# Attention products in halves of the TensorE array, and outputs that come out transposed

## The chip, the cores and the metric

The kernel runs on one core of one Trainium2 chip. The metric is the device time of one launch in microseconds: the median of the runs. Inside the core, TensorE multiplies, VectorE, ScalarE and GpSimd (POOL) work on elements, and DMA queues move data between device memory and the on-chip buffer SBUF. TensorE writes to PSUM, which has eight banks of 512 float32 columns on 128 partitions. The profile's PE is TensorE, PEld its loading of weights (the operand that stays in the array), DVE is VectorE and ACT ScalarE.

## The reference

A trunk of two residual layers for 256 tokens of 2048 features, all in float32. What matters here is the attention:

```python
# even layer, mixer A: 16 latent heads; an indexer of 16 heads of 64 features picks 64 keys per query
dots = relu(einsum('bqhd,bsd->bqhs', qi_b, k_idx))
score = einsum('bqh,bqhs->bqs', wi_b, dots) * idx_scale      # causal, then top-k
logits = einsum('bqhc,bqkc->bhqk', q_b, kv_sel) * att_scale + bias
o = softmax(logits) @ kv_sel, then @ w_uv                     # 64 features per head
# even layer, mixer B: 16 heads of 64 features, a window of 128 keys, two key/value heads, a sink logit
logits = q @ k / 8 + bias;  probs = softmax([logits, sink])[..., :-1];  o = probs @ v
# odd layer, mixer C: 32 heads of 64 features, causal, with a decay from forget gates
logits = q @ k / 8 + decay;  o = softmax(logits) @ v
# each layer:  x += concat(o) @ w_out;  x += conv_ffn(norm(x));  x += sigmoid(norm(x) @ w_gate) * (p @ w_proj)
```

## The kernel before

Tokens are handled in two blocks of 128 (`b` = 0, 1); in block `b` a query sees `n` = 128 or 256 keys. Weights come from device memory in pieces (`load`, L102), and `granule` splits each into two parts, `whi` on ScalarE (L114) and `wlo` on VectorE (L115). A large product is then three products in the parts, which `Acc.add` (L142) and the feed-forward part (L808, L810) issue. Products between activations in the attention stay in plain float32, and each of them appears in the trace as two instructions with a weight load each.

`attention` (L231) handles some heads of one token block. `head_groups` (L219) divides the heads into groups that fill one PSUM bank: four heads of 128 keys or two of 256. Where a head has 64 features, two heads share a tile of 128 partitions, and a group holds either the even heads (partitions 0 to 63) or the odd ones (64 to 127); the groups follow one another. For each group `front` makes the scores (L246) in the one bank of the ring `qk`, adds the bias or decay on VectorE, takes the maximum (L252), and exponentiates on ScalarE (L254) with the sums on the side. `back` transposes the probabilities (L263) into a bank of the ring `ax`, copies them out (L266), and multiplies them with the values (L269): the probabilities are the weights, the 64 columns of a value head stream, and the outputs [tokens, heads x 64] gather in the one bank `o`. The front of the next group is issued ahead of the back of the last. At the end VectorE takes the reciprocals of the sums (L282) and multiplies the outputs by them while it copies them out (L283). `transpose_split` (L165 to L171) transposes the outputs again, four 128x128 tiles per 512 columns (L169), and splits them for the output projection. The index scores (L462 to L473) have the same order of groups, with a relu in place of the softmax.

The eight banks are four rings: `mm` 3, `o` 1, `qk` 1, `ax` 3. The up-projections of the feed-forward part take banks from `mm` and `qk` in turn. `ple_project` (L752) multiplies the per-layer embedding before the feed-forward part, from two buffers of its own.

The program doesn't fix the order on each engine by its text alone: a planner orders the instructions by a simulated time and by priority. Attention is issued at a raised priority, so TensorE's order puts its pieces between the products of the projections, which fill the time in which other engines work on a score. Each engine then runs its list in order.

Of the kernel before, what the change touches and what calls it, by code (L numbers as in the profile page):

```python
# [16 lines left out]
P = 128  # L17
# [25 lines left out]
BANKS = dict(mm=3, o=1, qk=1, ax=3)  # L43
# [3 lines left out]
def trunk(ctx, tc, t, onehot, out):  # L47
# [20 lines left out]
    def rsqrt(dst, src, n, scale, post=1.0):  # L68
        """dst = post / sqrt(src * scale + EPS), by Newton from an exponent guess; [P, NT, n] or [P, NT]"""
# [54 lines left out]
    class Acc:  # L124
        """PSUM accumulators [tokens, ncols] of both token blocks for one column chunk."""
# [52 lines left out]
    def norm(gain, name, loaded=()):  # L178
        """Transposes of x * gain; 1 / rms is left to the caller (h.rstd), on the products."""
# [17 lines left out]
    def bcast_cols(dst, cols):  # L197
        """dst[:, token] = cols[block][token in block], on every partition of dst"""
# [6 lines left out]
    def transpose_to(dst, src, n, parts=P, scale=None, eng="v"):  # L205
        """dst [128, n*parts-token] <- n transposed [parts, 128] column tiles of src."""
# [12 lines left out]
    def head_groups(nh, n, halves):  # L219
        """Local head indices, as many as a PSUM bank holds; where two heads share a column tile  # L220
        (halves), the heads of the lower and the upper partitions go to different banks."""
        per = 512 // n
        if not halves:
            return [list(range(g, min(g + per, nh))) for g in range(0, nh, per)]
        gs = []
        for g in range(0, nh, 2 * per):
            m = min(g + 2 * per, nh)
            gs += [list(range(g, m, 2)), list(range(g + 1, m, 2))]
        return gs

    def attention(pool, heads, b, qk, logits, vv, y_out, halves, extra=0, mask=None):  # L231
        """Writes y_out [tokens, heads * 64] for token block b."""
# [4 lines left out]
        nl = sm.tile([P, 8], F32, tag="att_l", name="att_l", bufs=2)[:, :nh]  # L237

        def front(grp):
            per = len(grp)  # L240
            ps = psum("qk")
            s = pool.tile([P, 516], F32, tag="att_s", name="att_s", bufs=3)[:, :per * (n + extra)].rearrange("p (h c) -> p h c", h=per)
            for i, m in enumerate(grp):
# [3 lines left out]
            for i, m in enumerate(grp):  # L247
                logits(s[:, i, :], ps[:, i * n:(i + 1) * n], heads[m], b, n)
            if mask is not None:
                nc.vector.tensor_tensor(s[:, :, :n], s[:, :, :n], mask[:, None, :n].to_broadcast([P, per, n]), op=ALU.add)  # L250
            nm = sm.tile([P, 4], F32, tag="att_m", name="att_m", bufs=3)[:, :per]
            nc.vector.tensor_reduce(nm, s, axis=AX.X, op=ALU.max, negate=True)  # L252
            for i, m in enumerate(grp):
                nc.scalar.activation(s[:, i, :], s[:, i, :], AF.Exp, bias=nm[:, i:i + 1],  # L254
                                     accum_out=nl[:, m:m + 1])
            return s

        def back(grp, s):
            per = len(grp)
            pt = psum()  # L260
            for i in range(per):
                for kb in range(nk):
                    nc.tensor.transpose(pt[:, (i * nk + kb) * P:(i * nk + kb + 1) * P],  # L263
                                        s[:, i, kb * P:(kb + 1) * P], ident)
            pT = pool.tile([P, 512], F32, tag="att_p", name="att_p", bufs=2)
            nc.scalar.copy(pT[:, :per * n], pt[:, :per * n])  # L266
            for i, m in enumerate(grp):
                for kb in range(nk):
# [4 lines left out]
        grps = head_groups(nh, n, halves)  # L273
        prev = None
        for grp in grps:
            s = front(grp)
            if prev is not None:
                back(*prev)
            prev = grp, s
        back(*prev)  # L280
        rl = sm.tile([P, 8], F32, tag="att_r", name="att_r", bufs=2)[:, :nh]
# [8 lines left out]
    def ssq_heads(pool, ps, nh, dst):  # L290
        """dst [P, nh] = per-head sums of squares of ps [P, nh*64]."""
# [16 lines left out]
    # ======================= even layer: DSA + sliding window ====================  # L308
    def even_mixer(i, e):
        W = t["w_in_even"][e]  # L310
        with ExitStack() as es:
            ev = es.enter_context(tc.tile_pool(name="ev", bufs=1))
            def bias_tile(h0, nh):
                """[P, nh, 256]: column m of a row i is the bias of distance i + m - 127."""
# [5 lines left out]
            def key_bias(toe, m, n):  # L320
                """bias of the last n of 256 keys for head m of a bias tile, in the order of the keys"""
# [3 lines left out]
            # the first loads, in the order of their use  # L325
# [10 lines left out]
            # --- c_q  # L336
# [27 lines left out]
            # relative-position bias vectors: rv[h, m] = bias of distance m - 127  # L364
# [7 lines left out]
            for m in range(2):  # L372
                pr = psum()
                nc.tensor.matmul(pr[:16, :RV], tab[:, m * 16:(m + 1) * 16], oh[:, m, :], start=True, stop=True)
                rv = ev.tile([P, 516], F32, tag="att_s", name="rv", bufs=3)[:16, :RV]
# [3 lines left out]
            # --- c_kv, k_idx, w_idx  # L379
# [18 lines left out]
            for b in range(NT):  # L398
# [3 lines left out]
                # the index keys twice, so that both halves of the partitions hold them  # L402
# [14 lines left out]
            # --- index queries (features on partitions), scores, top-k masks  # L417
# [36 lines left out]
            with tc.high_priority(offset=PR):  # L454
                for b in range(NT):
                    n = P * (b + 1)
                    acc = ev.tile([P, S], F32, name=f"score{b}")
                    # causal mask first: keys after the query rank behind all others
# [3 lines left out]
                    for grp in head_groups(IDX_H, n, True):  # L462
                        pd = psum("qk")
                        for m, hh in enumerate(grp):
                            q0 = (hh % 2) * HD
                            nc.tensor.matmul(pd[:, m * n:(m + 1) * n], qiT[hh // 8][q0:q0 + HD, (hh % 8) // 2, b * P:(b + 1) * P],  # L466
                                             kiT[q0:q0 + HD, :n], start=True, stop=True)
                        rl = ev.tile([P, 516], F32, tag="att_s", name="relu", bufs=3)[:, :512]
                        nc.scalar.activation(rl, pd, AF.Relu)
                        for m, hh in enumerate(grp):  # L470
                            nc.vector.scalar_tensor_tensor(acc[:, :n], rl[:, m * n:(m + 1) * n],
                                                           wix[b][:, hh:hh + 1], acc[:, :n],
                                                           op0=ALU.mult, op1=ALU.add)  # L473
# [8 lines left out]
            # --- keys and values of the sliding window heads  # L482
# [27 lines left out]
            # --- values of the latent heads: kv @ w_uv  # L510
# [13 lines left out]
            # --- latent heads  # L524
            ya = {}

            def att_a(c):
# [10 lines left out]
                for b in range(NT):  # L538
# [5 lines left out]
                    if c % 2:  # L544
                        transpose_split(yT, c // 2, b, ya[b])

            # --- sliding window heads
# [15 lines left out]
            def att_b(c, qbT, rqs):  # L563
# [11 lines left out]
                for b in range(NT):  # L575
# [3 lines left out]
                    transpose_split(yT, 2 + c, b, y)  # L579
# [27 lines left out]
    # ============================ odd layer: forgetting attention ==================  # L607
    def odd_mixer(i, o):
        W = t["w_in_odd"][o]
        HDC = H_C * HD  # L610
        with ExitStack() as es:
# [44 lines left out]
            def att(g, qT, rqs, kT, v):  # L656
# [34 lines left out]
            # forget gates, heads on partitions  # L691
# [8 lines left out]
            # scratch for the gates, in the buffers of the first heads  # L700
# [11 lines left out]
            # log1p(e) = ln(u) + (e - (u - 1)) / u with u = fl(1 + e)  # L712
# [207 lines left out]
```

## Time and profile before

| | |
|---|---|
| median of 3 runs | 2465.46 us (2464.89 to 2466.26) |
| profiled execution, first to last instruction | 2464.3 us |
| TensorE busy | 2442.4 us, 99% |
| VectorE busy | 1659.9 us, 67% |
| ScalarE busy | 1278.1 us, 52% |
| GpSimd busy | 67.1 us, 3% |
| DMA, mean | 184 GB/s |

The page names no other time of the profiled execution than its span. The even layer's attention lies between some 62 and 345 us, its feed-forward part and gate follow up to 1190, the odd layer's attention lies between 1270 and 1565. A record of a product lasts from its start to a modelled end, and the next product starts earlier than that, so how long TensorE is held by one is read from start to start.

### The profile page before, as it was taken

The numbers are of one execution on the slowest core, as the hardware profiler recorded it, in microseconds if no ns is written. First come the engines' busy times: TensorE is split into PE (matmuls) and PEld (weight loads), VectorE is DVE, ScalarE is ACT, GpSimd is POOL, SyncE is SP. The second block draws the span as 40 slices with busy tenths as digits, with TensorE's granted clock in tenths as the row PEclk, the third lists the DMA queues.
The fourth block names the chain that finished last, engine by engine and source line by source line (L and its number), as shares of the span: only waits on it lengthen the run. The fifth ranks groups of instructions, "written<-read, shape, count | busy, mean of one in ns | idle before, by whom it ended". The sixth has DMA issues, their size and how long they took to land.

```text
span 2464.3 us, 32544 instructions
## 1 busy us (share of the span) xinstructions
PE 2442.4 (99%) x12594; PEld 2056.8 (83%) x12594; DVE 1659.9 (67%) x2536; ACT 1278.1 (52%) x1977; POOL 67.1 (3%) x138
## 2 busy tenths in 40 slices
PE   8999999999999999999999999999999999999999
PEld 6888888888888888888788888888888888888887
DVE  7677776777646777556676566677777457777564
ACT  6546555555434555444554555455555345555443
POOL 0000000000000000000021110000000000000000
PEclk9999999999999999999999999999999999999999
DMA  8444437555556555656555554566555565556664
GB/s 272 133 138 155 137 105 251 188 185 192 188 189 198 177 194 178 206 194 225 170 197 172 172 173 155 159 213 203 180 196 180 191 210 171 190 186 193 203 199 158
DMA packets 334000, 454.26 MB, mean 184 GB/s; under 512 B 15807, under 2 KB 210019, under 8 KB 333844
## 3 DMA queue, kind: packets, MB, share of 16 engines
q1 hardware_dynamic: 332468, 447.89, 56.0%
q0 software_dynamic: 1376, 4.28, 0.4%
q8 instruction: 99, 1.62, 0.3%
q14 instruction: 57, 0.47, 0.1%
HBM read 445.76 MB, written 6.37 MB: 183 GB/s over the span
## 4 chain that ended last, share of the span: by engine, by line
PE 90%; issue 7%; DMA 2%; DVE 1%; ACT 0%; POOL 0%; SPq 0%; DVEq 0%; ACTq 0%; POOLq 0%
PE ps_mm L142 44%; PE ps_mm L808 13%; PE ps_qk L808 13%; PE ps_mm L810 7%; PE ps_qk L810 6%; PE ps_qk L246 2%; PE ps_o L269 1%; PE ps_ax L263 1%; PE ps_ax L169 1%; PE ps_ax L209 1%; DMA pled<-y 1%; PE ps_qk L466 1%; DMA gain<-in_attn_norm_dram 0%; PE ps_ax L428 0%; DVE wlo L115 0%
## 5 line engine op out<-in xcount | busy, mean ns | idle before, releaser
L115 DVE TENSOR_TENSOR wlo<-raw,whi 128x1024 fp32r<-128x1024 f32 (+1 forms) x846 | 981.6, 1169 | 602.3 <-ACT whi L114 589.3
L114 ACT CAST whi<-raw 128x1024 fp32r<-128x1024 f32 (+1 forms) x846 | 848.0, 1007 | 707.9 <-PE ps_mm L142 500.0
L808 PE MATMUL ps_qk<-nf,whi 128*128 128x512 f32 x1376 | 491.5, 398 | 0.0
L808 PE MATMUL ps_mm<-nf,whi 128*128 128x512 f32 x1376 | 489.4, 398 | 0.6 <-ACT y L771 0.6
L810 PE MATMUL ps_qk<-nf,wlo 128*128 128x256 f32 x1376 | 386.2, 281 | 1.4 <-DVE wlo L115 1.4
L810 PE MATMUL ps_mm<-nf,wlo 128*128 128x256 f32 x1376 | 380.8, 281 | 0.0
L142 PE MATMUL ps_mm<-whi,n 128*128 128x512 f32 (+2 forms) x1088 | 334.7, 387 | 0.8 <-ACT n L121 0.5
L808 PEld LDWEIGHTS ps_qk<-nf,whi 128*128 128x128 f32 x1376 | 258.5, 188 | 64.0 <-ACT whi L114 0.5
L808 PEld LDWEIGHTS ps_mm<-nf,whi 128*128 128x128 f32 x1376 | 256.4, 188 | 61.7 <-ACT y L771 1.3
L142 PE MATMUL ps_mm<-whi,glo 128*128 128x512 f32 x688 | 268.3, 390 | 0.0
L142 PE MATMUL ps_mm<-wlo,ghi 128*128 128x512 f32 x688 | 268.0, 389 | 0.0
L142 PE MATMUL ps_mm<-whi,ghi 128*128 128x512 f32 x688 | 266.3, 390 | 0.0
L810 PEld LDWEIGHTS ps_mm<-nf,wlo 128*128 128x128 f32 x1376 | 259.8, 189 | 3.3
L810 PEld LDWEIGHTS ps_qk<-nf,wlo 128*128 128x128 f32 x1376 | 259.8, 189 | 2.7 <-DVE wlo L115 2.2
L142 PEld LDWEIGHTS ps_mm<-whi,n 128*128 128x128 f32 x1088 | 201.2, 190 | 39.5 <-issue 1.4
L142 PE MATMUL ps_mm<-wlo,n 128*128 128x512 f32 (+2 forms) x544 | 209.6, 386 | 0.4 <-DVE wlo L115 0.3
L821 ACT ACTIVATE u<-un,cw 128x256 f32<-128x256 f32 x172 | 78.5, 503 | 166.1 <-DVE un L817 166.1
L142 PE MATMUL ps_mm<-whi,np 128*128 128x512 f32 x512 | 158.8, 390 | 0.0
L142 PEld LDWEIGHTS ps_mm<-whi,glo 128*128 128x128 f32 x688 | 129.1, 188 | 26.8
L142 PEld LDWEIGHTS ps_mm<-wlo,ghi 128*128 128x128 f32 x688 | 129.2, 188 | 26.7
L142 PEld LDWEIGHTS ps_mm<-whi,ghi 128*128 128x128 f32 x688 | 128.9, 188 | 26.5
L142 PEld LDWEIGHTS ps_mm<-wlo,n 128*128 128x128 f32 x544 | 103.2, 190 | 23.1 <-issue 3.0
(222 smaller groups left out, 2561.5 us busy)
## 6 DMA issues: line engine op xcount, KB each, us to landing
raw<-in_w_up_dram SPq DMA_DIRECT2D x168, 1024.0 KB, 5.3
raw<-in_w_down_dram SPq DMA_DIRECT2D x80, 1024.0 KB, 5.1
raw<-in_w_in_odd_dram SPq DMA_DIRECT2D x48, 1024.0 KB, 5.1
raw<-in_w_ple_gate_dram SPq DMA_DIRECT2D x32, 1024.0 KB, 5.1
raw<-in_w_out_even_dram SPq DMA_DIRECT2D x16, 1024.0 KB, 5.1
raw<-in_w_out_odd_dram SPq DMA_DIRECT2D x16, 1024.0 KB, 5.1
raw<-in_a_w_uq_dram SPq DMA_DIRECT2D x8, 1024.0 KB, 5.5
raw<-in_w_in_even_dram SPq DMA_DIRECT2D x8, 1024.0 KB, 5.3
```

The costliest lines, as they stand in the source:

```text
L114: nc.scalar.copy(hi, v[:, z:z + m])
L115: nc.vector.tensor_tensor(lo, v[:, z:z + m], hi.bitcast(F32), op=ALU.subtract)
L142: nc.tensor.matmul(self.ps[b], l, r[i], start=self.n[b] == 0, stop=self.n[b] == 3 * self.total - 1)
L169: nc.tensor.transpose(pt[:, i * P:(i + 1) * P], src[:, i * P:(i + 1) * P], ident)
L209: nc.tensor.transpose(pt[:, i * parts:(i + 1) * parts], src[:, i * P:(i + 1) * P], ident[:parts, :parts])
L246: nc.tensor.matmul(ps[:, i * n:(i + 1) * n], lt, rh, start=c == 0, stop=c == len(pairs) - 1)
L263: nc.tensor.transpose(pt[:, (i * nk + kb) * P:(i * nk + kb + 1) * P], s[:, i, kb * P:(kb + 1) * P], ident)
L269: nc.tensor.matmul(o[:, m * HD:(m + 1) * HD], pT[:, (i * nk + kb) * P:(i * nk + kb + 1) * P], vv(heads[m], kb), start=kb == 0, stop=kb == ...
L466: nc.tensor.matmul(pd[:, m * n:(m + 1) * n], qiT[hh // 8][q0:q0 + HD, (hh % 8) // 2, b * P:(b + 1) * P], kiT[q0:q0 + HD, :n], start=True, ...
L808: nc.tensor.matmul(pu[z], hi[k][:, cols], h.both(k0 + k), start=k0 + k == 0, stop=k0 + k == KD - 1, skip_group_check=True)
L810: nc.tensor.matmul(pu[z][:, :S], lo[k][:, cols], h.rhs(k0 + k)[0], start=False, stop=k0 + k == KD - 1, skip_group_check=True)
L821: nc.scalar.activation(u[:, z, :], src, AF.Copy, scale=cw[:, 2, blk:blk + 1])
```

## The change

The scores of the even and the odd heads are issued in turn, one head of the lower partitions, one of the upper, into two banks; so are the index scores. The probabilities are divided by their sums before they are transposed, one multiplication per head. In the product with the values the operands change places: the values are the weights (64 columns), the transposed probabilities stream (128 columns), and the outputs come out as [64 features, tokens], an even head on the lower 64 partitions of `o` and its odd neighbour on the upper ones. So the outputs are transposed already, a copy brings them to SBUF, and `split_to` splits them from there; the four transposes per tile are gone. The ring `qk` has two banks and `ax` two; the buffers `att_s` are four. `ple_project` is called in the feed-forward part's pool, ahead of its norm, and its buffers are those that the first gate tiles use later. The diff without its removed comments, cut:

```diff
-BANKS = dict(mm=3, o=1, qk=1, ax=3)
+BANKS = dict(mm=3, o=1, qk=2, ax=2)
...
-            gs += [list(range(g, m, 2)), list(range(g + 1, m, 2))]
+            gs.append([list(range(g, m, 2)), list(range(g + 1, m, 2))])
...
+    def alternate(grps):
+        return [(g, i, grps[g][i]) for i in range(len(grps[0])) for g in range(len(grps))]
...
+        def front(grps):
+            per = len(grps[0])
+            pss = [psum("qk") for _ in grps]
...
+            for g, i, m in alternate(grps):
                 pairs = qk(heads[m], b, n)
                 for c, (lt, rh) in enumerate(pairs):
-                    nc.tensor.matmul(ps[:, i * n:(i + 1) * n], lt, rh, start=c == 0, stop=c == len(pairs) - 1)
+                    nc.tensor.matmul(pss[g][:, i * n:(i + 1) * n], lt, rh, start=c == 0, stop=c == len(pairs) - 1)
...
+            lo, hi = min(min(g) for g in grps), max(max(g) for g in grps) + 1
+            nc.vector.reciprocal(rl[:, lo:hi], nl[:, lo:hi])
+            for grp, s in zip(grps, ss):
+                for i, m in enumerate(grp):
+                    nc.vector.tensor_scalar(s[:, i, :n], s[:, i, :n], rl[:, m:m + 1], None, op0=ALU.mult)
...
+            at = {m: (g, i) for g, i, m in alternate(grps)}
+            for m in sorted(at):
+                if m % 2:
+                    continue
                 for kb in range(nk):
-                    nc.tensor.matmul(o[:, m * HD:(m + 1) * HD],
-                                     pT[:, (i * nk + kb) * P:(i * nk + kb + 1) * P],
-                                     vv(heads[m], kb), start=kb == 0, stop=kb == nk - 1)
+                    for mm in (m, m + 1):
+                        g, i = at[mm]
+                        z = (mm % 2) * HD
+                        nc.tensor.matmul(o[z:z + HD, m // 2 * P:(m // 2 + 1) * P], vv(heads[mm], kb),
+                                         pTs[g][:, (i * nk + kb) * P:(i * nk + kb + 1) * P],
+                                         start=kb == 0, stop=kb == nk - 1, skip_group_check=True)
...
-        nc.vector.reciprocal(rl, nl)
-        nc.vector.tensor_tensor(y_out.rearrange("p (h d) -> p h d", h=nh), o[:, :nh * HD].rearrange("p (h d) -> p h d", h=nh),
-                                rl[:, :, None].to_broadcast([P, nh, HD]), op=ALU.mult)
+        nc.vector.tensor_copy(y_out, o[:, :nh * HD])
+
+    def split_to(h, j, b, src):
+        split_evict(h.t[j][:, :, 0, b * P:(b + 1) * P], h.t[j][:, :, 1, b * P:(b + 1) * P],
+                    src.rearrange("p (a c) -> p a c", a=4))
...
-                    transpose_split(yT, g, b, ys[b][g], "ax" if g == 3 else "mm")
+                    split_to(yT, g, b, ys[b][g])
...
-        pT.hi = work.tile([P, 2, S], F32R, tag="pT_hi", name="pT_hi", bufs=1)
-        pT.lo = work.tile([P, 2, S], F32R, tag="pT_lo", name="pT_lo", bufs=1)
+        pT.hi = ff.tile([P, 2, S], F32R, tag="ghi0", name="pT_hi")
+        pT.lo = ff.tile([P, 2, S], F32R, tag="glo0", name="pT_lo")
```

## Rows read from the trace of the kernel before

**Rows 1.** The page: span, busy time of the engines, TensorE's clock in forty slices.
```profile
span 2464.3 us, 32544 instructions
PE 2442.4 (99%) x12594; PEld 2056.8 (83%) x12594; DVE 1659.9 (67%) x2536; ACT 1278.1 (52%) x1977; POOL 67.1 (3%) x138
...
PEclk9999999999999999999999999999999999999999
```

**Rows 2.** Windows: stretch, length, then busy us per engine, clock, DMA share, GB/s.
```profile
270.00:345.00 75.00, 75.00 (x412) 62.23 (x413) 51.91 (x84) 38.55 (x89) 4.38 (x22) 1.00 0.35 118
...
395.00:1190.00 795.00, 795.00 (x4120) 677.27 (x4119) 533.00 (x700) 406.35 (x543) 0.30 (x1) 1.00 0.60 194
...
1270.00:1521.00 251.00, 251.00 (x1236) 206.13 (x1234) 156.32 (x278) 128.41 (x225) 35.06 (x57) 1.00 0.53 174
```

**Rows 3.** Waits of TensorE, the longest: us in total, times, longest.
```profile
PE ps_ax L169 <- DVE xg L188: 7.0, 2, 6.2
```

**Rows 4.** Single lines: count, ns min/median/max, first and last start us, shapes.
```profile
L466 PE MATMUL ps_qk<-kiT,qiT x64: 272/374/631, 69.4 to 120.5; 64*128 64x128 f32 x32, 64*128 64x256 f32 x32
L246 PE MATMUL ps_qk<-kT,qT x128: 272/374/480, 1272.6 to 1546.5; 64*128 64x128 f32 x64, 64*128 64x256 f32 x64
L269 PE MATMUL ps_o<-v,att_p x192: 218/275/323, 1286.1 to 1560.6; 128*128 128x64 f32 x192
L169 PE MATMUL ps_mm<-ident,yc x24: 271/272/329, 1524.7 to 1533.4; 128*128 128x128 f32 x24
L169 PE MATMUL ps_ax<-ident,yA x16: 270/273/328, 200.8 to 272.6; 128*128 128x128 f32 x16
L763 PE MATMUL ps_ax<-ident,xg x8: 270/272/273, 344.8 to 1598.3; 128*128 128x128 f32 x8
```

**Rows 5.** Chain of waits, one head group of the odd layer: start us, us, what.
```profile
1438.40 1.09 PE ps_qk L246 x8
...
1447.06 5.04 PE ps_mm L142 x22
1452.10 0.84 PE ps_o L269 x8
...
1454.16 0.63 PE ps_qk L246 x2
...
1467.85 0.44 PE ps_ax L263 x4
1468.30 1.06 PE ps_qk L246 x4
```

**Rows 6.** Timeline of TensorE around a 64-row run: start us, us, instruction.
```profile
1272.25 0.39 PE L142 MATMUL ps_mm<-wlo,n 128*128 128x512 f32 x1
1272.57 1.16 PE L246 MATMUL ps_qk<-kT,qT 64*128 64x128 f32 x8
1273.65 0.73 PE L142 MATMUL ps_mm<-whi,n 128*128 128x512 f32 x2
1274.22 0.40 PE L142 MATMUL ps_mm<-wlo,n 128*128 128x512 f32 x1
```

**Rows 7.** Timeline of TensorE behind products of 32 output columns.
```profile
1232.32 0.62 PE L202 MATMUL ps_ax<-ident,rstd 128*32 128x128 f32 x4
1232.88 0.50 PE L142 MATMUL ps_mm<-wlo,n 128*128 128x512 f32 x1
1233.22 0.64 PE L142 MATMUL ps_mm<-whi,n 128*128 128x512 f32 x2
```

**Rows 8.** Weight loads by shape: busy us, mean ns of one, idle before.
```profile
L269 PEld LDWEIGHTS ps_o<-v,att_p 128*128 128x128 f32 x192 | 25.0, 191 | 2.1 <-ACT att_p L266 0.4
...
L699 PEld LDWEIGHTS ps_ax<-n,whi 128*32 128x32 f32 x32 | 3.5, 108 | 0.2
```

**Rows 9.** VectorE by shape: busy us, mean ns of one, idle before.
```profile
L816 DVE TENSOR_TENSOR un<-ps_mm,un 128x256 f32<-128x256 f32 x86 | 36.0, 419 | 3.3 <-ACT un L815 3.3
...
L504 DVE TENSOR_SCALAR xg<-xg,hr 128x128 f32<-128x128 f32 x4 | 0.9, 281 | 0.0
```

More of the change, by code (lines that the diff above doesn't have):

```diff
@@ L223, in head_groups @@
         if not halves:
-            return [list(range(g, min(g + per, nh))) for g in range(0, nh, per)]
+            return [[list(range(g, min(g + per, nh)))] for g in range(0, nh, per)]
         gs = []
@@ L237, in attention @@
         nl = sm.tile([P, 8], F32, tag="att_l", name="att_l", bufs=2)[:, :nh]
[L239 to L243, printed above, removed]
+        rl = sm.tile([P, 8], F32, tag="att_r", name="att_r", bufs=2)[:, :nh]
+        def front(grps):
+            per = len(grps[0])
+            pss = [psum("qk") for _ in grps]
+            ss = [pool.tile([P, 516], F32, tag="att_s", name="att_s", bufs=4)[:, :per * (n + extra)]
+                  .rearrange("p (h c) -> p h c", h=per) for _ in grps]
+            for g, i, m in alternate(grps):
@@ L252, in front @@
[L252 to L261, printed above, removed]
-                for kb in range(nk):
[L263 to L268, printed above, removed]
-                    nc.tensor.matmul(o[:, m * HD:(m + 1) * HD],
-                                     pT[:, (i * nk + kb) * P:(i * nk + kb + 1) * P],
-                                     vv(heads[m], kb), start=kb == 0, stop=kb == nk - 1)
@@ L273, in attention @@
-        grps = head_groups(nh, n, halves)
+                    nc.tensor.matmul(pss[g][:, i * n:(i + 1) * n], lt, rh, start=c == 0, stop=c == len(pairs) - 1)
+            for grp, ps, s in zip(grps, pss, ss):
+                for i, m in enumerate(grp):
+                    logits(s[:, i, :], ps[:, i * n:(i + 1) * n], heads[m], b, n)
+                if mask is not None:
+                    nc.vector.tensor_tensor(s[:, :, :n], s[:, :, :n], mask[:, None, :n].to_broadcast([P, per, n]), op=ALU.add)
+                nm = sm.tile([P, 4], F32, tag="att_m", name="att_m", bufs=4)[:, :per]
+                nc.vector.tensor_reduce(nm, s, axis=AX.X, op=ALU.max, negate=True)
+                for i, m in enumerate(grp):
+                    nc.scalar.activation(s[:, i, :], s[:, i, :], AF.Exp, bias=nm[:, i:i + 1],
+                                         accum_out=nl[:, m:m + 1])
@@ new lines, in front, with back @@
+            lo, hi = min(min(g) for g in grps), max(max(g) for g in grps) + 1
+            nc.vector.reciprocal(rl[:, lo:hi], nl[:, lo:hi])
+            for grp, s in zip(grps, ss):
+                for i, m in enumerate(grp):
+                    nc.vector.tensor_scalar(s[:, i, :n], s[:, i, :n], rl[:, m:m + 1], None, op0=ALU.mult)
+            return ss
+        def back(grps, ss):
+            per = len(grps[0])
+            pTs = []
+            for s in ss:
+                pt = psum()
+                for i in range(per):
+                    for kb in range(nk):
+                        nc.tensor.transpose(pt[:, (i * nk + kb) * P:(i * nk + kb + 1) * P],
+                                            s[:, i, kb * P:(kb + 1) * P], ident)
+                pT = pool.tile([P, 512], F32, tag="att_p", name="att_p", bufs=2)
+                nc.scalar.copy(pT[:, :per * n], pt[:, :per * n])
+                pTs.append(pT)
+            at = {m: (g, i) for g, i, m in alternate(grps)}
+            for m in sorted(at):
+                if m % 2:
+                    continue
+                for kb in range(nk):
+                    for mm in (m, m + 1):
[4 more added lines that the diff above has]
+                                         start=kb == 0, stop=kb == nk - 1, skip_group_check=True)
@@ L461, in even_mixer @@
                                             fill=CAUSAL, base=0, channel_multiplier=1)
[L462 to L464 removed]
+                    for grps in head_groups(IDX_H, n, True):
+                        pds = [psum("qk") for _ in grps]
+                        for g, m, hh in alternate(grps):
                             q0 = (hh % 2) * HD
[L466 removed]
+                            nc.tensor.matmul(pds[g][:, m * n:(m + 1) * n], qiT[hh // 8][q0:q0 + HD, (hh % 8) // 2, b * P:(b + 1) * P],
                                              kiT[q0:q0 + HD, :n], start=True, stop=True)
[L468 to L473, printed above, removed]
+                        for grp, pd in zip(grps, pds):
+                            rl = ev.tile([P, 516], F32, tag="att_s", name="relu", bufs=4)[:, :512]
+                            nc.scalar.activation(rl, pd, AF.Relu)
+                            for m, hh in enumerate(grp):
+                                nc.vector.scalar_tensor_tensor(acc[:, :n], rl[:, m * n:(m + 1) * n],
+                                                               wix[b][:, hh:hh + 1], acc[:, :n],
+                                                               op0=ALU.mult, op1=ALU.add)
                     m8 = ev.tile([P, 8], F32, tag="m8", name="m8", bufs=2)
```

25 lines of the change are left out of this document (10 added, 15 removed).

## The prediction

> **What bounds the kernel now.** [...] The stages come next, because a share over the whole span could hide one with another limit: TensorE shows no idle time in the sliding-window part of the even layer (75.0 of 75.0 us), in the feed-forward part (795.0 of 795.0) and in the odd layer's attention (251.0 of 251.0), while VectorE has 51.9 of 75 and 156.3 of 251 [rows 2]. The waits confirm it: the longest single wait of TensorE, for xg of a norm, is 7.0 us in two pieces [rows 3]. So what TensorE is spared in the attention comes off the span as long as another engine doesn't take over, and nothing that changes in the feed-forward part can gain.
>
> Busy time overlaps within TensorE (an instruction's record runs on while the next streams), so I price by the distance between starts. In the chain of one head group of the odd layer a run of four 64-row score products of 256 columns takes 1.06 us and a run of two 0.63, so one takes 0.215 and the run has 0.20 of its own; eight of 128 columns take 1.09, of which 0.89 is left after the same 0.20: 0.112 each; eight values products take 0.84, 0.105 each; four transposes 0.44 where nothing is in their way, 0.11 each [rows 5].
>
> **What a change of array shape costs.** Around a 64-row run the timeline shows more than its own 0.20: the 512-column product ahead of it starts 0.32 us before the run where 0.23 is usual, and the two products behind it take 0.57 to the next start instead of 0.45 [rows 6]. So a run costs 0.09 + 0.20 + 0.11 = 0.40 us beside its columns. The same shows when TensorE leaves a product of 32 columns: the four 128-column products take 0.56 instead of 0.44, and the next 512-column product 0.34 instead of 0.23 [rows 7].
>
> **The parts, in TensorE time.** An fp32 product is two instructions, so counts are instructions.
>
> 1. Output transposes: 64 go (24 into mm and 40 into ax, of which one row of each stands) [rows 4], at 0.11 each: -7.0 us. The split that followed them reads SBUF instead of PSUM and keeps its size.
>
> 2. Fewer 64-row runs. Going through the products that rows 4 count, from the first at 69.4 us to the last at 1546.5, I find 51 runs: 12 for the index scores, 12 for the sliding window, 27 in the odd layer. Paired groups leave 6 + 6 + 12 = 24. 27 x 0.40 = -10.8. Ends: zero, if the planner splits the pairs again, and -10.8.
>
> 3. Overlap of the two halves. 128 of these instructions have 256 columns, 128 have 128 [rows 4]: 64 and 64 in the odd layer, 32 and 32 in the index scores, and as many again in the sliding window, whose row isn't repeated. No row shows two halves at work at once, as each run stays in one half. Ends: no overlap, 0; full overlap, half of 128 x 0.215 and half of 128 x 0.112: -20.9. What stands between is the weight load. A values product of 64 columns takes 0.105 us although the transposes with twice its columns take 0.11 [rows 5], so some 0.107 is the time of loading 128 columns. If loads remain one behind another, 256-column products fall to 0.112 and 128-column ones stay. I take that: 128 x (0.215 - 0.112) = -13.2.
>
> 4. Values products. Before 384 (192 and twice 96; the row of the 192 stands) [rows 4] at 0.105: 40.3 us. After as many, with 64 columns to load and 128 to stream. A 32-column load lasts 108 ns and a 128-column one 191 [rows 8]; 83 ns for 96 columns make some 0.055 for 64, just under the pace that full overlap gives, 0.112 / 2 = 0.056, so that loads would not hold it up. So with overlap 384 x 0.056 = 21.5, -18.8 us; without it 384 x 0.112 = 43.0, +2.7. I take the first, as the two column halves touch no common output partition.
>
> 5. New column runs: 4 x 3 for the latent heads, 2 x 3 for the sliding window, 4 x 3 in the odd layer, 30 in all. Each pays the 0.09 into it, 0.09 out of it and 0.11 of the next load, and 0.05 for its first load of half the columns: 0.34. +10.2. Ends: +6 where a column run touches a 64-row run and shares the drain, +15 where the planner splits them in half as many again.
>
> 6. VectorE gets 128 multiplications of probabilities, 64 of 128 columns at 0.28 us (the row of the same shape) and 64 of 256 at up to 0.42 (the nearest, a tensor-tensor of that size) [rows 9]: 45 us. The multiplication of the outputs becomes a copy of equal size. In the odd layer 22 us go into 251 with 95 idle: hidden, behind TensorE. In the sliding-window stretch 11 us come to 51.9 while TensorE's 75 shrink by some 9: 63 of 66. That is too tight for an engine that runs in order and also makes wlo, for which TensorE waits. Ends: 0, and 20 if the stretch grows by the 11 instead of shrinking by the 9. I take +5.
>
> 7. At nothing: the second qk bank in the feed-forward part (TensorE has no gap to lose there); the ax ring of two (a bank is held for 0.44 us of transposes and a copy); the projection of the embedding, whose buffers now lie in the feed-forward pool. Its transposes start at 344.8 us at the earliest [rows 4], about when the last attention output has left, so it still covers the norm. Without that cover the norm's gaps would grow, by up to 4 us.
>
> Sum: -7.0 - 10.8 - 13.2 - 18.8 + 10.2 + 5 = -34.6. The profiled execution has 2464.3 us from first to last instruction; the median of the timed runs is 2465.46, 1.2 more, which I add: 2464.3 - 34.6 + 1.2 = 2431 us.
>
> **The rivals.**
>
> A. Weight loads of different halves overlap too, and VectorE keeps up: -7.0 - 10.8 - 20.9 - 18.8 + 10.2 = -47.3, 2418. For it: 64-row loads sit in separate partitions. Against it: the narrow margin of VectorE. [...]
>
> B. Only one of the two overlaps. Rows alone: -7.0 - 10.8 - 13.2 + 2.7 + 10.2 + 2 = -16.1, 2449. Columns alone: -7.0 - 10.8 - 18.8 + 10.2 + 4 = -22.4, 2443. For it: no row of the trace has two products in one array; both would be new.
>
> C. Neither overlaps: the change doesn't do what it says. -7.0 - 10.8 + 2.7 + 10.2 + 1 = -3.9, 2462. The runs that merge then pay for the runs that come.
>
> D. Column products whose loads are not hidden. Loading must wait for the product in flight, and each values instruction takes 0.107 + 0.055 = 0.16: 384 x 0.16 = 61.4, +21.1; -7.0 - 10.8 - 13.2 + 21.1 + 10.2 = +0.3, 2466. [...]
>
> E. Slower: the ax ring. A pair takes both banks for its probabilities, TensorE runs in order, and a third transpose must wait until ScalarE, behind a cast of a microsecond or eight exponentials, has copied the first out. There are 48 such probability tiles and about 40 of queries and keys in the attention stages. It decides from 35 us / 88 = 0.4 us of wait each; with 1 us, 2431 + 88 = 2519, with 0.6, 2484. Against it: the planner puts some 20 products, 5 us, between a score run and its transposes [rows 5], and the same can lie between a transpose and the next.
>
> **How the numbers follow.** Forecast 0.45 (2424 to 2440), A 0.15, B 0.17, C 0.12, D 0.04, E 0.07. About 0.2%, 5 us, is what a measurement of this kernel tells from no change: faster means below 2460.5, slower above 2470.4. Faster: forecast, A, B and a quarter of C, 0.80. Same: two thirds of C, most of D, 0.11. Slower: E and what is left, 0.09. The range reaches from below A to C, 2412 to 2462, and leaves out E, D, half of C and the tail of A.
>
> **What would show it.** Right: 64-row runs of 8 and 16 instructions, the 256-column ones at half the distance, 0.112; values products of 128x128 in runs of eight that take about 0.45 us beside their fixed cost; 64 transposes less; TensorE still idle for under 30 us. Wrong in step 3 or 4: distances of 0.215 or 0.112 within such runs. Wrong in 6: TensorE idle between 270 and 345 us, released by VectorE's att_s or wlo. E would show as idle before transposes, released by ScalarE's att_p. The forecast as a whole is wrong if the odd layer's attention, 251 us now, loses less than 10.

## The result and the profile after

The changed kernel takes 2451.65 us (median; 2445.56 to 2451.85, four runs) against 2465.86 for the kernel before on the same chip (2464.89 to 2468.27, four runs): a ratio of 0.9935, 95% interval 0.9921 to 0.9948. It is faster by 14 us where 34.6 were forecast. The profiled execution lasts 2450.1 us from first to last instruction.

The page after, against [rows 1]: TensorE still bounds the kernel, with nine tenths or more of its full clock granted in every slice (a digit 9 stands for 90% or more).

```profile
span 2450.1 us, 32617 instructions
PE 2426.1 (99%) x12530; PEld 2019.7 (82%) x12530; DVE 1687.4 (69%) x2670; ACT 1266.4 (52%) x1977; POOL 63.1 (3%) x138
...
PEclk9999999999999999999999999999999999999999
```

The windows after (columns as in [rows 2]); the first is the index stage, the others have the times of [rows 2]. TensorE has no idle time in the sliding-window stretch although VectorE went from 51.9 to 63.1 of 75 us there. The work has moved forward a little (the sliding window's scores run from 246.7 to 294.5 us, before from 263.3 to 324.7), but between 240 and 345 us TensorE has no idle time either. In the index stage it is idle for 4.3 us, where the kernel before had 1.4.

```profile
62.00:126.00 64.00, 59.66 (x380) 50.68 (x380) 45.87 (x145) 34.92 (x79) 0.00 (x0) 0.96 0.41 124
...
270.00:345.00 75.00, 75.00 (x435) 60.26 (x434) 63.06 (x115) 42.77 (x92) 2.85 (x16) 1.00 0.41 130
395.00:1190.00 795.00, 793.07 (x4064) 670.05 (x4063) 529.38 (x695) 396.03 (x540) 0.30 (x1) 1.00 0.60 191
...
1270.00:1521.00 251.00, 251.00 (x1273) 200.00 (x1272) 180.57 (x349) 139.79 (x253) 29.73 (x57) 1.00 0.55 179
```

TensorE's waits after: beside the one of [rows 3] there is a new one, for the window keys (line 529). Line numbers are those of the changed kernel from here on.

```profile
PE ps_ax L169 <- DVE xg L188: 6.1, 1, 6.1
PE ps_ax L209 <- DVE xg L529: 3.7, 1, 3.7
```

The timeline of TensorE in the odd layer after (start, us, instruction), which answers to [rows 5] and [rows 6]. Sixteen 64-row products of 128 columns last as long as eight did before. But those of 256 columns still come four by four, each run as long as before: 1.06 us from start to start, 0.215 a product.

```profile
1296.30 1.09 PE L292 MATMUL ps_o<-att_p,v 128*64 128x128 f32 x16
...
1347.48 1.16 PE L253 MATMUL ps_qk<-kT,qT 64*128 64x128 f32 x16
1354.24 1.13 PE L253 MATMUL ps_qk<-kT,qT 64*128 64x256 f32 x4
1355.73 1.13 PE L253 MATMUL ps_qk<-kT,qT 64*128 64x256 f32 x4
```

Summed from start to start over both traces, TensorE's time changes so:

| TensorE, after minus before | us |
|---|---|
| output transposes (64 instructions) | -6.9 |
| 64-row products with the 0.20 that ends each run | 53.5 to 40.6: -12.9 |
| values products with the 0.20 that ends each run | 41.6 to 26.5: -15.1 |
| products of the down-projection (2064 instructions, line 142) | 469.6 to 481.9: +12.3 |
| the group of query products in the index stage, with the new wait | +4.4 |
| the rest: products beside the new column runs some +4, the up-projection of the feed-forward part +3.1, all others some -3 | +4.0 |

The up-projection's pace differs between two traces of one kernel. From 363 to 610 us TensorE has 1383 instructions in the trace of the result, and 1411 in the second trace of the same kernel (the first experiment below):

```profile
363.00:610.00 247.00, 245.76 (x1383) 211.96 (x1382) 182.75 (x254) 136.07 (x198) 2.70 (x5) 1.00 0.64 202
363.00:610.00 247.00, 245.80 (x1411) 213.91 (x1411) 185.49 (x260) 138.72 (x203) 2.70 (x5) 1.00 0.65 204
```

All products of the up-projection take 976.1 us in the one and 971.4 in the other. With 32 and with 96 bytes added (below) they take 970.2 and 971.1, in the other traces with two separate score banks 975.4 to 976.1, in the traces with one buffer for the pair (below) 972.0 to 972.9, and in those of the kernel before 972.2 to 973.6. Why is open. Two times can so differ by some 5 us without an edit behind it, and where an effect below is of that size, the time of the products concerned stands beside it.

The down-projection is the surprise. It has the same instructions in both kernels; the longest undisturbed piece of its first half shows the pace (the chain of waits: start, us, what, count). Before, 27.92 / 123 = 227.0 ns a product:

```profile
1053.85 27.92 PE ps_mm L142 x123
```

After, 27.75 / 119 = 233.2 ns:

```profile
1047.59 27.75 PE ps_mm L142 x119
```

### The profile page after: what moved, and what is told of

It reads as the page before. It is cut to its first block, busy times and chain, and to the rows that moved or that the text cites. A ratio compares the mean times of both kernels' runs of the same rounds, so it can differ in the third digit from the quotient of the medians.

```text
span 2450.1 us, 32617 instructions
## 1 busy us (share of the span) xinstructions
PE 2426.1 (99%) x12530; PEld 2019.7 (82%) x12530; DVE 1687.4 (69%) x2670; ACT 1266.4 (52%) x1977; POOL 63.1 (3%) x138
## 4 chain that ended last, share of the span: by engine, by line
PE 90%; issue 7%; DVE 1%; DMA 1%; ACT 0%; POOL 0%; DVEq 0%; SPq 0%; POOLq 0%; ACTq 0%
PE ps_mm L142 44%; PE ps_mm L835 13%; PE ps_qk L835 13%; PE ps_mm L837 7%; PE ps_qk L837 7%; PE ps_qk L253 2%; PE ps_o L292 1%; PE ps_ax L278 1%; PE ps_ax L209 1%; PE ps_ax L169 1%; PE ps_ax L452 0%; DMA pled<-y 0%; PE ps_qk L490 0%; DMA gain<-in_attn_norm_dram 0%; DVE wlo L115 0%
## 5 line engine op out<-in xcount | busy, mean ns | idle before, releaser
L835 PE MATMUL ps_qk<-nf,whi 128*128 128x512 f32 x1376 | 546.9, 399 | 0.9 <-ACT whi L114 0.9
L835 PE MATMUL ps_mm<-nf,whi 128*128 128x512 f32 x1376 | 546.4, 399 | 0.4 <-ACT y L797 0.4
L837 PE MATMUL ps_mm<-nf,wlo 128*128 128x256 f32 x1376 | 386.7, 281 | 0.0
L142 PEld LDWEIGHTS ps_mm<-whi,np 128*128 128x128 f32 x512 | 96.0, 188 | 19.8
```

The source lines that it names most:

```text
L142: nc.tensor.matmul(self.ps[b], l, r[i], start=self.n[b] == 0, stop=self.n[b] == 3 * self.total - 1)
L835: nc.tensor.matmul(pu[z], hi[k][:, cols], h.both(k0 + k), start=k0 + k == 0, stop=k0 + k == KD - 1, skip_group_check=True)
L837: nc.tensor.matmul(pu[z][:, :S], lo[k][:, cols], h.rhs(k0 + k)[0], start=False, stop=k0 + k == KD - 1, skip_group_check=True)
```

## Experiments: the pace of the down-projection

A product here has a split activation as the weights (`ghi` or `glo`) and a piece of the streamed matrix as the moving operand (`whi` or `wlo`). What differs between the kernels is where `ghi` and `glo` lie: a fourth buffer of 32 bytes for `att_m` moved all but the first pair of them by 32 bytes (the buffers of `pT`, gone from the pool ahead, are 4096 bytes, a multiple of 256). Of each address I name the remainder by 256: `whi`, `wlo` and the activations of most other projections lie at 128, `ghi` and `glo` at 128 before and at 160 after. Unused bytes in the feed-forward pool, ahead of them, move them and leave the order of instructions on every engine as it was, but for the one instruction on GpSimd that writes them.

**The changed kernel once more** (no edit).

> The changed kernel once more, as the base of the runs beside it. Both theories: 2451 us, 14 less than the kernel before (ratio 0.994), with the three products of the down-projection (ghi and glo as weights) at 232 to 234 ns from start to start, where the kernel before has 227.

2447.24 us (2446.07 to 2447.93), ratio 0.9925 (0.9912 to 0.9937): the result stands.

**The changed kernel, 32 bytes added** (`ghi` at 192).

```diff
-            pd = ple_project(i, ff)
+            pd = ple_project(i, ff); nc.gpsimd.memset(ff.tile([P, 8], F32, name="pad"), 0.0)
```

> The changed kernel with 32 unused bytes in the feed-forward pool, behind the buffers of the embedding, so that the gate tiles ghi and glo move from byte 32 of a 64-byte line to byte 0; every engine's order is the same. Theory 1 (where the weights of a product begin in a 64-byte line sets the pace of 512-column products): back to 227 ns in the down-projection, 2064 products by 6 ns, so 12 us less than the changed kernel, 2439. Theory 2 (the slower pace comes from what other engines and DMAs do beside it): nothing changes, 2451.

2446.26 us (2445.03 to 2451.12), pace still 233.0 ns (a piece of 119 in 27.73 us). A multiple of 64 bytes is not enough; this form of the theory fell. Its line of 64 bytes was the author's assumption, and no run shows one.

**The kernel before, 32 bytes added** (`ghi` at 160, as after), and nothing of the change.

```diff
-            ff = es.enter_context(tc.tile_pool(name=f"ff{i}", bufs=1))
+            ff = es.enter_context(tc.tile_pool(name=f"ff{i}", bufs=1)); nc.gpsimd.memset(ff.tile([P, 8], F32, name="pad"), 0.0)
```

> The kernel before with 32 unused bytes ahead of everything in the feed-forward pool, so that ghi and glo move from byte 0 to byte 32 of a 64-byte line; same orders. Theory 1: the down-projection goes from 227 to 233 ns, 12 us more, 2478. Theory 2: 2465, no change.

2476.66 us (2474.98 to 2479.47), ratio 1.0045 (1.0032 to 1.0058): 11.6 us slower by the address alone, with the same piece at 28.70 / 123 = 233.3 ns:

```profile
1058.12 28.70 PE ps_mm L142 x123
```

**The changed kernel, 96 bytes added** (`ghi` at 0): the same edit with `[P, 24]`.

> The changed kernel with 96 unused bytes in the feed-forward pool, so that all gate tiles begin at a multiple of 128 bytes, as they did in the kernel before; same orders on all engines. Theory 1b (weights that do not begin at a multiple of 128 bytes slow the product; 32 and 64 bytes beyond one cost the same): the down-projection at 227 ns again, 12 us less than the changed kernel's 2447 of the same chip, 2435. Theory 2 (in the changed kernel it is not the address): 2446, as with 32 bytes.

2444.29 us (2443.13 to 2447.31), pace 232.3 ns: a multiple of 128, or of 256, isn't what counts either. What was left was the place that the streamed operand has, 128.

```profile
1045.03 27.64 PE ps_mm L142 x119
```

**The kernel before, 128 bytes added** (`ghi` at 0): the edit of the kernel before with `[P, 32]`. **The changed kernel, 224 bytes added** (`ghi` at 128 again): with `[P, 56]`.

> The kernel before with 128 unused bytes ahead of the feed-forward pool: the gate tiles begin at a multiple of 256 bytes, where in the kernel before they, the split weights and the normed activations all begin 128 bytes beyond one. Theory 1c (the pace is 227 ns only where the array's weights begin at the same offset within 256 bytes as the operand that streams, 128): 232 ns in the down-projection, as in the changed kernel with 96 bytes, 2064 products by 5 ns, 2476. Rival (in the changed kernel with 96 bytes, where this offset was also 0, the pace of 232 ns came from something other than the address): 227 ns, 2465.

> The changed kernel with 224 unused bytes: all gate tiles 128 bytes beyond a multiple of 256, as in the kernel before; same orders. Theory 1c: 227 ns, 9 to 10 us less than with 96 bytes, 2435. Rival: 232 ns, 2444.

The first took 2475.14 us (2474.62 to 2476.75), 11 more than before; its piece took 28.59 / 123 = 232.4 ns. The second took 2436.12 (2435.53 to 2436.72), ratio 0.9880 (0.9864 to 0.9897), some 11 less than the changed kernel as it was, and the pace is back at 226.9:

```profile
1041.77 27.00 PE ps_mm L142 x119
```

Against 96 bytes it is 8.2 less: the down-projection takes 469.2 us instead of 480.3, as the theory has it, but the up-projection takes 975.6 instead of 971.1.

**The kernel before, 256 bytes added** (`[P, 64]`), and **the kernel before with the streamed weights, all split activations of the projections, `ghi` and `glo` moved together by 32 bytes** (all at 160).

```diff
-    wp = ctx.enter_context(tc.tile_pool(name="wp", bufs=3))
+    wp = ctx.enter_context(tc.tile_pool(name="wp", bufs=3)); nc.gpsimd.memset(wp.tile([P, 8], F32, name="pad", bufs=1), 0.0)
```

> The kernel before with 256 unused bytes at the head of the feed-forward pool, so that the split activations of the down-projection move by 256 bytes and keep their offset within 256. Theory (what counts is the offset within 256 bytes): 227 ns from start to start in the down-projection, and the time of the kernel before within 2 us. Rival (any move away from the old place costs, or the added bytes themselves do): 232 ns and some 10 us more, as with 32 and 128 bytes.

> The kernel before with 32 unused bytes at the head of the pool of the streamed weights, so that the streamed weights, the split activations of all projections and those of the down-projection all move by 32 bytes together (160 within 256). Theory (what counts is that both operands of a product stand at the same offset within 256 bytes): 227 ns in the down-projection, and the time of the kernel before within 3 us. Rival (what counts is the place itself, 128 within 256): all split products, some 9000 of 512 columns, take 231 to 233 ns instead of 227, which is 35 to 55 us more.

2466.19 us (ratio 1.0001, 0.9992 to 1.0011) and 2465.17 (0.9999, 0.9990 to 1.0009): no change in either, and 227 ns in both. With `ghi` at 160, where it cost 11.6 us above, it costs nothing once the streamed weights are at 160 as well:

```profile
1054.62 27.93 PE ps_mm L142 x123
```

So it is not the place of one operand but whether both stand at the same remainder. The traces of the result hold a second witness. In the kernel before, `cq_hi` (the low-rank queries) and `pT_hi` lay at 96 against the weights' 128, and their products have a median distance of 234 ns; after the change both lie at 128, and it is 228. Within the changed kernel the products of the first `ghi` and `glo` buffers, which lie at 128, average 229 ns from one to the next, those of the others 233.

## Experiments: the order of the scores

By the partitions of their operands, the 64-row products after the change form 41 runs, not 24, and at 256 columns (of a run's two-instruction products, L on the lower half, U on the upper) twelve are LL and eleven UU, three LLUU, one LULU: the two banks of the ring come free at different times, and the planner issues each half as soon as its bank is there. The text alternates; TensorE's list doesn't.

**One two-bank buffer for a pair**, so that both halves come free together. The index scores have the same edit, a lone `qk` bank elsewhere is the first half of such a buffer, and the first kernel has the 32 bytes as well.

```diff
-            pss = [psum("qk") for _ in grps]
+            pss = psum_pair()[:len(grps)]
...
+    def psum_pair():
+        t2 = pp.tile([P, 1024], F32, tag="qk", name="ps_qk", bufs=1)
+        return [t2[:, :512], t2[:, 512:]]
```

> The changed kernel with the 32 bytes, and with both score banks of a pair as one buffer of two banks, which comes free as a whole, so that the planner issues the heads of a pair in turn (14 runs of 8 and one of 16 for 256 columns instead of 29 runs of one half or of one half after the other). Theory 1 (halves overlap where they are issued in turn, and the changed kernel loses it for 256 columns because the planner splits the pairs): 128 instructions go from 0.215 to about 0.11 us, 12 us, and 16 runs less at 0.40, 6 us: 18 less than the run with the 32 bytes alone, 2421. Rival (256-column products gain nothing from turns, as their loads or reads collide, or the single buffer costs what is won): within 5 us of that run, 2434 to 2444.

2434.84 us (2432.39 to 2437.08), 11.4 less than without it, where 18 were expected. The 64-row products take 29.1 us instead of 40.6. All their runs are now LULU or longer, 25 in all.

The same with 96 and with 224 bytes:

> The same 96 bytes with both score banks of a pair as one buffer. Theory 1b: 12 us less than the run with 32 bytes and the pair buffer, 2423; and 12 less than the run with 96 bytes alone, as between the two runs with 32 bytes. Theory 2: 2435.

> The same 224 bytes with both score banks of a pair as one buffer. Theory 1c: 9 to 10 us less than with 96 bytes and the pair buffer, 2422; rival: 2432. Against the run with 224 bytes alone, 13 us less.

2431.70 (2428.11 to 2434.64), 12.6 less than with 96 bytes alone, but only 3.1 less than the pair with 32 bytes: 96 bytes don't mend the address. And 2421.96 (2420.34 to 2426.44), 14.2 less than with 224 bytes alone, ratio to before 0.9825 (0.9810 to 0.9841). In the last one's timeline eight products of 256 columns last as long as four did:

```profile
1410.06 1.16 PE L259 MATMUL ps_qk<-kT,qT 64*128 64x128 f32 x16
1418.18 1.13 PE L259 MATMUL ps_qk<-kT,qT 64*128 64x256 f32 x8
...
1427.99 1.09 PE L298 MATMUL ps_o<-att_p,v 128*64 128x128 f32 x16
```

**Is the strict alternation needed?** The 224-byte pair kernel with both halves one behind the other (L L U U) into the pair of banks, in the index scores too:

```diff
-            for g, i, m in alternate(grps):
+            for g, i, m in sorted(alternate(grps)):
```

> As the run before, but each pair's scores are issued for all heads of the lower half and then for all of the upper one. Theory (halves overlap where they are issued in turn; in sequence they meet only where TensorE looks a few instructions ahead, as the columns did): of the 256 instructions' gain of 20 us about half is lost, 7 to 12 us more than the run with the pair buffer in turn. Rival (the gain of the pair buffer came from fewer runs alone): within 3 us of it.

2426.15 us (2423.06 to 2427.57) against 2421.96 beside it: 4.2 more, with ranges that overlap; the 64-row products take 32.3 us instead of 29.3, 3.0 more. That is about what the rival expected, but not for its reason, since halves in sequence overlap too. The products of 256 columns don't mind (1.07 us for eight in the chain of waits); sixteen of 128 take 1.64 us instead of 1.09, about halfway to two runs of eight:

```profile
1413.30 1.64 PE ps_qk L259 x16
...
1421.97 1.07 PE ps_qk L259 x8
```

## Experiments: values products, multiplications, keys

**Values products, all even heads and then all odd ones**, with 96 bytes.

```diff
-            for m in sorted(at):
-                if m % 2:
-                    continue
+            for m in sorted(at, key=lambda m: (m % 2, m)):
...
-                    for mm in (m, m + 1):
+                    for mm in (m,):
```

> The changed kernel with 96 bytes, in which the values products of one run are issued for all even heads and then for all odd ones, so that the two column halves meet only once a run. Theory (the two column halves overlap, and that is what the values products gained): 384 instructions at up to 0.107 instead of some 0.06 us, 16 to 18 us more than with the 96 bytes alone. Rival (they gained from loading 64 columns instead of 128, whatever the order): less than 4 us more.

2455.90 us (2455.30 to 2457.74), 11.6 more than with 96 bytes alone, ratio 0.9961 (0.9948 to 0.9974). Of that the values products have 8.2 us (34.7 instead of 26.5), and 4.3 are the up-projection's (975.4 instead of 971.1), which the edit doesn't touch. So the overlap of the column halves is real, and alternation is worth some 8 us over an order in which the halves still meet, between the two expectations: a run of sixteen takes 1.58 where alternation takes 1.09.

```profile
1450.52 1.58 PE L290 MATMUL ps_o<-att_p,v 128*64 128x128 f32 x16
```

In the records of such a run the first four starts stand alone, 109 to 160 ns apart; in the middle come eight that share the array, the first of the odd heads 6 ns behind the fifth of the even ones; the last four stand alone again, 109 apart. The latent heads, with two and two, lose almost nothing (6.6 to 6.8 us in sum).

**The 128 multiplications of the probabilities left out**, with 96 bytes.

```diff
-            for grp, s in zip(grps, ss):
-                for i, m in enumerate(grp):
-                    nc.vector.tensor_scalar(s[:, i, :n], s[:, i, :n], rl[:, m:m + 1], None, op0=ALU.mult)
```

> The changed kernel with 96 bytes without the 128 multiplications of the probabilities by the reciprocal sums (the softmax is left unnormalized). Theory (VectorE has room for them, its 45 us lie beside TensorE's work): within 2 us of the run with the 96 bytes. Rival (they hold the sliding-window stretch back, as step 6 of the forecast has it): 5 us less, up to 10.

2453.68 us (2443.29 to 2454.78), not less than with them. It settles nothing: with other work on VectorE the planner made another order, in which fourteen column runs are a single product (three with 96 bytes alone) and the sliding window's values products take 2.5 us more; and the up-projection takes 975.6 us instead of 971.1.

**The window keys ahead of the index scores**, in the 224-byte pair kernel: the block of 26 lines that begins here moves ahead of the indexer's scores and top-k.

```diff
+            o5 = Q_LORA + KV_LORA + HD + IDX_H + H_B * HD
+            ps = moving(W, o5, 4 * HD, h.lhs, KD)
...
-            o5 = Q_LORA + KV_LORA + HD + IDX_H + H_B * HD
-            ps = moving(W, o5, 4 * HD, h.lhs, KD)
...
```

> The kernel with 224 bytes and the pair buffer, with one move: the window keys (their projection, their sums of squares, their scaling and transposes) are issued ahead of the index scores instead of behind them. Theory: the 4.1 us that TensorE waits at 116.7 us for the keys' xg, and the slow clock behind it, come from VectorE's top-k rounds standing in front of the keys' scaling; with the keys ahead of them the wait goes, 4 to 8 us less than the 2422 of that kernel, 2414 to 2418. Rival: the keys only move the wait (the top-k result, or the index queries, become what is late), and the time stays within 3 us of 2422.

2421.69 us (2420.81 to 2422.85): no gain; the rival was right. The wait was first seen in the changed kernel. There VectorE's list is a mixture: the rounds that pick the top keys (lines 501 and 502), the splitting of weights (115) and the small steps of the keys' norm (73 to 80), which the keys' scaling must follow. Its timeline:

```profile
112.17 0.41 DVE L501 MAX8 m<-score 128x8 f32<-128x256 f32 x1
112.51 0.27 DVE L326 TENSOR_SCALAR hrt<-sk,rstd 128x2 f32<-128x2 f32 x1
112.69 0.08 DVE L502 MATCH_VALUE_LOAD score<-m,score 128x8 f32 x1
112.76 0.41 DVE L502 MATCH_REPLACE8 score<-m,score 128x256 f32<-128x256 f32 x1
113.08 0.15 DVE L73 TENSOR_SCALAR rq_v<-hrt 128x4 f32<-128x4 f32 x1
113.20 0.43 DVE L501 MAX8 m<-score 128x8 f32<-128x256 f32 x1
```

With the keys early, TensorE waits earlier, in the trace's list of waits, for the index scores' relu and again for the keys:

```profile
PE ps_ax L215 <- DVE xg L503: 2.4, 1, 2.4
...
PE ps_qk L522 <- ACT relu L526: 1.2, 1, 1.2
```

and its windows show what VectorE does there: from 96 to 105 us it has no free time. Behind the wait the granted clock is 0.56 from 105 to 108 us, where the changed kernel has 0.51 from 120.8 to 127.6. The group of query products that had the wait takes 15.7 us instead of 20.8, but the 64-row products take 33.5 instead of 29.3.

```profile
96.00:99.00 3.00, 3.00 (x18) 2.19 (x16) 3.00 (x12) 0.65 (x1) 0.00 (x0) 1.00 0.89 248
99.00:102.00 3.00, 1.40 (x12) 0.69 (x8) 3.00 (x19) 1.40 (x3) 0.00 (x0) 1.00 0.26 101
102.00:105.00 3.00, 0.92 (x4) 0.56 (x4) 3.00 (x16) 1.19 (x4) 0.00 (x0) 1.00 0.00 0
105.00:108.00 3.00, 2.42 (x8) 2.14 (x9) 2.83 (x9) 3.00 (x13) 0.00 (x0) 0.56 0.00 0
```

VectorE is busy throughout this short stretch, so the order of its pieces seems only to choose who waits. Less work on VectorE there was not tried.

## Why the prediction was wrong

Direction and range were right, the size was not: 14 us instead of 34.6. The range held by luck in so far as its largest loss, in the down-projection, was in none of its terms. The sign that the prediction set for the forecast as a whole did not come: from the first to the last score of the odd layer it is 260.7 us (1267.1 to 1527.8) where it was 273.9 (1272.6 to 1546.5), 13 less.

**Step 7 failed.** It put everything in the feed-forward part "at nothing", and looked at banks and buffers as resources only. One more buffer of 32 bytes moved the weights of the down-projection off the streamed operand's remainder, and 2064 products took 6 ns more each, 12.3 us. Shown: the same cost appears in the kernel before without the change, goes when the remainder is restored, and doesn't come when both operands move.

**Steps 2 and 3 failed at their stated lower end**, "if the planner splits the pairs again". It split those of 256 columns, so the only products that step 3 wanted halved mostly were not: the odd layer's took 17.5 us before and 17.1 after. The runs fell from 51 to 41, not to 24. With the pair buffer the odd layer's fall to 8.5, and the 11 to 14 us come back.

**Step 3's choice between loads that queue and loads that overlap was wrong too, in the other direction.** The 128-column products of the odd layer went from 8.68 to 4.37 us, loads included: rival A's mechanism. In the 224-byte pair kernel all 64-row products take 29.3 us instead of 53.5; without the 26 fewer runs at 0.20 that is -19, near A's -20.9 and not the -13.2 forecast. In the trace of the result the two halves start 7 ns apart, and the sixteen loads of such a run, of 187 ns each (median), take 0.97 us together:

```profile
L253 PEld LDWEIGHTS ps_qk<-kT,qT x128: 182/187/189, 1267.1 to 1527.5; 64*128 64x128 f32 x128
...
1347.48 0.97 PEld L253 LDWEIGHTS ps_qk<-kT,qT 64*128 64x128 f32 x16 [0.35 <-issue]
```

**Step 4 held, with step 5.** Values products fell by 15.1 us with the ends of 31 column runs inside (30 were forecast). Rival D is out: the two halves start 7 ns apart, the next pair starts 109 ns after the last (160 after the first of a run), although each load of 64 columns lasts 137. The records of the changed kernel's loads and products:

```profile
L292 PEld LDWEIGHTS ps_o<-att_p,v x192: 132/137/138, 1289.5 to 1550.6; 128*64 128x64 f32 x192
L292 PE MATMUL ps_o<-att_p,v x192: 272/273/324, 1289.5 to 1550.7; 128*64 128x128 f32 x192
```

**Step 6 wasn't paid.** The multiplications were sized right (38 us busy, 45 forecast), but TensorE is busy for 75.0 of 75.0 us in the sliding-window stretch, and from 240 to 345 us as well. VectorE's shortage came where the forecast had not looked, in the index stage, where the scores now end earlier and the top-k rounds meet the norm of the keys: +4.4 us. That this meeting is caused by the second bank of the ring was not tried alone.

**Step 1 held** (-6.9 for -7.0), and rival E didn't come: no wait of TensorE for a copied probability reaches 0.4 us.

By the terms: without the 5 of step 6 the forecast was -39.6; the down-projection gives back 12.3, the index stage 4.4, the up-projection 3.1, and steps 2 to 5 lack 5.5 (-27.1 for -32.6, the remaining 0.9 of the table's rest counted with them). That leaves -14.3, for a profiled span that is 14.2 shorter. With the address and the pairs mended the same change is worth 42 us (2421.96).

One row was misread, without weight in the sum: the 7.0 us of [rows 3] are the sum of two waits, of which the longest is 6.2. Nor does the digit 9 of the clock in [rows 1] say full clock: in that trace the granted clock is 0.55 from 120.8 to 124.2 us (the last section shows the window).

## What to carry to other kernels

A change that adds, drops or moves an on-chip buffer shifts buffers allocated behind it (here 32 bytes took an untouched product from 227 to 233 ns), so compare the start-to-start pace of untouched products before believing that a distant stage is unchanged. Where two pieces of work must stand next to each other on an engine, tie them to one resource that comes free once: writing them in turn isn't enough where a planner orders. And price a halved cost from the engine's list as it will be issued, not from the text.

## What the runs showed of the hardware that was not expected

- A 512-column split product starts 227 ns after the last where weights and moving operand stand at the same remainder by 256 bytes, and 232 to 234 ns where the weights are off by 32, 64 or 128 (at 96, 160, 192 and 0 against 128). Products against a streamed operand at another remainder agree (160 against 160: 227.1). Why is not known, and other shapes weren't tried.
- Products in the two row halves or the two column halves start 7 ns apart, although a load lasts 187 ns in the row halves and 137 in the column halves (medians), and two together take what one took (sixteen 64-row products of 128 columns 1.16 us, as eight did).
- They need not alternate strictly: two and two lose next to nothing (eight products of 256 columns 1.07 us, where four of one half take 1.06), and in a run of eight and eight TensorE starts the second half's products before the first half's have ended (1.58 us for sixteen values products, against 1.09 alternating).
- Behind the new wait of 3.7 us in the index stage the granted clock is 0.51 for 6.8 us, where the trace of the kernel before has 0.55 for 3.4. That the wait does this is not shown: with 256 bytes added the kernel before, whose longest wait there is 0.7 us, has 0.50 for 6.8 us as well.

```profile
116.00:120.80 4.80, 1.09 (x5) 0.56 (x3) 4.73 (x23) 0.00 (x0) 0.00 (x0) 1.00 0.69 218
120.80:127.60 6.80, 6.17 (x18) 4.88 (x19) 1.53 (x5) 5.72 (x18) 0.00 (x0) 0.51 0.00 1
```

the kernel before:

```profile
120.80:124.20 3.40, 3.40 (x11) 2.69 (x11) 1.92 (x4) 3.37 (x13) 0.00 (x0) 0.55 0.00 0
124.20:127.60 3.40, 3.40 (x20) 2.84 (x19) 3.26 (x9) 3.35 (x8) 0.00 (x0) 1.00 0.00 0
```

and the kernel before with 256 bytes added:

```profile
118.90:125.70 6.80, 6.80 (x20) 4.95 (x20) 3.67 (x10) 6.03 (x20) 0.00 (x0) 0.50 0.00 1
```
